# Two column groups of an output projection as a seven-product pair, woven with the groups around it

## The chip, the cores and the metric

The kernel runs on one core of one Trainium2 chip. The metric is the device time of one execution in microseconds; the time before is the median of three runs. A profile is one further execution, recorded instruction by instruction.

## The reference

One layer of a streaming-encoder trunk on 256 tokens of width 2048, all in float32: a SwiGLU block, LayerNorm, a mixer, LayerNorm, a second SwiGLU block, LayerNorm, and a gated per-layer input. Cut to what matters here, the mixer's end is

```
merged = sigmoid(ga) * (y_m @ w_up_m) + sigmoid(gb) * (y_sb @ w_up_sb)   # 256 x 2048
mix    = merged @ w_out                                                  # w_out 2048 x 2048
x      = layer_norm(ALPHA * x + mix, ln2_g, ln2_b)
x      = layer_norm(ALPHA * x + 0.5 * swiglu(x), ln3_g, ln3_b)
```

## The kernel before

**Matmuls.** Tokens lie in two halves of 128 (t = 0, 1). The width is handled in column groups of 512 and the contracted dimension in chunks of 512, each chunk as two weight tiles of 256 rows. A *unit* (the main loop, L1301 to L1329) is one weight tile against one token half: six matmuls of 128 x 512, because both operands are split into a high part (type float32r) and a low part, the rest, and three of the four cross products are kept (L1319 to L1321), for each of two blocks of 128 rows.

**Weights.** A weight tile is loaded from memory into a `raw` tile (SP's queue, L1238, 512 KB). ScalarE casts it into the high part (L1264), VectorE subtracts to get the low part (L1268). This *split* runs some weights ahead; `HELD` says for each mode how many raw tiles and how many splits may be held, and near a stage boundary `SPLIT_EDGE` allows 11 splits.

**Activations.** A finished 128 x 512 tile is turned by four transposes on TensorE (L293), then cast by ScalarE (L295) and subtracted by VectorE (L300). An `ActT` holds the turned tiles.

**Plain groups and pairs.** `group` makes a plain column group: 8 weight tiles, each used by two units, 16 units. `seven` makes a *pair*: two column groups at once with seven products where the plain way has eight. In a chunk, tokens, contracted rows and columns each have two halves; sums of quarters of the activations (the *forms*) are multiplied with sums of quarters of the weights. A chunk needs seven units, each with a weight of its own to split, so that a pair has 28 units. The weight sums are made in place on the raw tiles: on VectorE (`plus`, L366) or by a load from memory that adds to what lies there (`plus_load`, issued by GpSimd, L372). `both7` combines the products on VectorE (L420, L426) and ScalarE (L436, L439). The forms are made by `form_turn`: four VectorE operations of 128 x 256 (L310 to L314), then two casts on ScalarE (L287) and two subtractions on VectorE (L288) for each chunk; for them a whole copy of the turned tile is kept (L299).

**Order.** The program is a list of units and of other steps, laid out in Python. `weave` puts a side list evenly between the units of a main list. What follows a unit's last matmul (`done`) is issued at once; later steps go to a planner (`Sched`) with a due time in planned microseconds, such as `DELAY["form"]`. Each engine then takes its queue in that order, and waits where something is not there yet.

**The stretch in question.** The last woven part ends with `ups(2)`. Then come `bring_back` (the residual rows return from memory, four loads of 512 KB), the turns of the first three merged groups, and:

```
    program.extend(ups(3))
    ...
    for g in range(4):
        pairs = group(w_out, range(0, D, 2 * P), g * COL, COL, mergedT, out_done(g))
        if g == 3:
            program.extend(flat(pairs[:-SKEW]) + skewed(pairs[-SKEW:]))
        else:
            program.extend(flat(pairs))
        if g == 1:
            program.append(norm2.load)
```

`ups(3)` is the last group of the two up projections (16 units); `up_done` multiplies by the gate (L1068), adds the two branches (L1070) and, for g = 3, plans its turn. `out_done` adds a group of `mix` to the residual rows (L1123) and takes LayerNorm statistics (L496). After the last group `Norm.finish` aggregates (L502), normalises (L508), and `Norm.turn` transposes the rows (L519) for the second SwiGLU. `skewed` puts the last six weight tiles' first token half ahead of the second, so that the first half can be normalised early.

Of the kernel before, what the change touches and what calls it, by code (L numbers as in the profile page):

```python
# [13 lines left out]
P = 128  # L14
S = 256
TT = S // P
D = 2048
# [6 lines left out]
COL = 512  # L24
# [2 lines left out]
TEMP_BUFS = 6  # L27


HELD = {"ffn": (11, 6), "mix": (6, 6), "woven": (9, 6), "wide": (11, 6)}  # L30
RAW_EDGE, SPLIT_EDGE = 4, 11
EDGE = 6

AHEAD = 3
PSUM_BUFS = 8
SKEW = 6

HEAD = 20

# [67 lines left out]
class ActT:  # L107


    def __init__(self, alloc, forms=None, later=False):  # L110
        self.alloc, self.soon = alloc, forms is not None and not later
        self.forms, self.whole = forms, {}
        self.tiles = {}
        self.left = {}

    def get(self, c, tt):
        if (c, tt) not in self.tiles:
# [62 lines left out]
def flat(pairs):  # L180
    return [u for p in pairs for u in p]


def skewed(pairs):
    return [p[0] for p in pairs] + [p[1] for p in pairs]
# [3 lines left out]
def kernel(  # L189
# [7 lines left out]
    x, out = x[0], out[0]  # L197
    p = p[0, 0]
    w_in, w_out, w_up_m, w_up_sb = w_in[0], w_out[0], w_up_m[0], w_up_sb[0]
# [9 lines left out]
    sched = Sched()  # L209
    temps = [0]  # L210

    def temp():
        sched.until(lambda: temps[0] < TEMP_BUFS)
        temps[0] += 1
        return temp_pool.tile([P, COL], F32, name="temp", tag="temp")

    def drop(n=1):
        temps[0] -= n
# [71 lines left out]
    def transposed(src, act, c, t):  # L290
        ps = misc([P, 4, P])
        for k in range(4):
            nc.tensor.transpose(ps[:, k], src[:, k * P:(k + 1) * P], ident[:])  # L293
        dst = act.get(c, t)
        nc.scalar.copy(dst[:, 0], ps[:])  # L295
        if act.soon:
            if c not in act.whole:
                act.whole[c] = big()
            nc.scalar.copy(act.whole[c][:, t * COL:(t + 1) * COL], ps.rearrange("q k s -> q (k s)"))  # L299
        nc.vector.tensor_tensor(out=dst[:, 1], in0=ps[:], in1=dst[:, 0], op=ALU.subtract)  # L300
        act.mark(c, t, 4)
        if act.soon and all(act.ready(c, h) for h in range(TT)):
            sched.spawn(form_turn(act, c), DELAY["form"] + 5.0 * c)

    def form_turn(act, c):

        a = [act.whole[c][:, t * COL:(t + 1) * COL] for t in range(TT)]
        s12, s34 = temp(), temp()
        l, r = slice(0, 2 * P), slice(2 * P, 4 * P)
        nc.vector.tensor_tensor(out=s12[:, l], in0=a[1][:, r], in1=a[1][:, l], op=ALU.subtract)  # L310
        nc.vector.scalar_tensor_tensor(out=s12[:, r], in0=s12[:, l], scalar=-1.0, in1=a[0][:, l],  # L311
                                       op0=ALU.mult, op1=ALU.subtract)
        nc.vector.tensor_tensor(out=s34[:, l], in0=a[0][:, l], in1=a[1][:, l], op=ALU.subtract)
        nc.vector.tensor_tensor(out=s34[:, r], in0=a[0][:, r], in1=s12[:, r], op=ALU.add)  # L314
        yield 4.0
        for h, src in enumerate((s12, s34)):
            dst = act.forms.get(c, h)
            split_psum(dst[:, 0], dst[:, 1], src.rearrange("q (k s) -> q k s", s=P))
            drop()
            act.forms.mark(c, h, 4)  # L320
# [18 lines left out]
    def group(w, rows, col0, cols, act, done):  # L339

        accs = [{} for _ in range(TT)]
        pairs = []
        for i, r in enumerate(rows):
            tile = plain(rows_of(w, r, col0, cols))
            pairs.append([Unit(tile, t, accs[t], act, r // COL, r % COL // P,
                               i == 0, i == len(rows) - 1, done) for t in range(TT)])
        return pairs
# [59 lines left out]
    def in_line(pairs):  # L407

        out = []
        for head, first, then in pairs:  # L410
            at = max(len(out) - 4, 0)
            out = out[:at] + head + out[at:] + first + then
        return out

    def both7(w, ca, cb, act, dest, ready, loaded):

        r, held = {}, {}

        def put(k, t, a, b, op):
            nc.vector.tensor_tensor(out=r[k, t], in0=a, in1=b, op=op)  # L420

        def rest():
            u = r[0, 1]
            put(0, 1, held[7], u, ALU.add)
            z = r[1, 1] = dest(1, 1)
            nc.vector.scalar_tensor_tensor(out=z, in0=u, scalar=-1.0, in1=held[5],  # L426
                                           op0=ALU.mult, op1=ALU.subtract)
            ready(1, 1)
            return
            yield  # L430

        def done(m, ps):
            held[m] = ps
            if m == 1:
                r[0, 1] = dest(0, 1)
                nc.scalar.copy(r[0, 1], ps)  # L436
            elif m == 2:
                r[0, 0] = dest(0, 0)
                nc.scalar.copy(r[0, 0], ps)  # L439
                ready(0, 0)  # L440
            elif m == 6:
                r[1, 0] = dest(1, 0)
                put(0, 1, ps, r[0, 1], ALU.add)
                put(1, 0, held[5], r[0, 1], ALU.add)
                sched.spawn(rest(), DELAY["rest"])
            elif m == 4:
                sched.until(lambda: (1, 1) in r)
                put(0, 1, ps, r[0, 1], ALU.add)
                ready(0, 1)
            elif m == 3:  # L450
                put(1, 0, ps, r[1, 0], ALU.subtract)
                ready(1, 0)

        return seven(w, ca, w, cb, D, COL, act, done, loaded)

    program = []

    def mode(name):
        program.append(Mode(name))
# [6 lines left out]
    class Norm:  # L466
# [47 lines left out]
        def turn(self, t, c):  # L514

            xs, act = xres(t, c * COL), self.act
            ps = misc([P, 4, P])
            for k in range(4):
                nc.tensor.transpose(ps[:, k], xs[:, k * P:(k + 1) * P], ident[:])  # L519
            if act.soon:  # L520
                if c not in act.whole:
                    act.whole[c] = big()
                whole = act.whole[c][:, t * COL:(t + 1) * COL]
            else:
                whole = temp()[:]
            whole = whole.rearrange("q (k s) -> q k s", s=P)
            for k in range(4):
                i = 4 * c + k
                activate(whole[:, k], ps[:, k], ACT.Identity, scale=self.gb[:, i:i + 1], bias=self.gb[:, 16 + i:17 + i])
            dst = act.get(c, t)  # L530
            split_psum(dst[:, 0], dst[:, 1], whole)
            act.mark(c, t, 4)
            if not act.soon:
                drop()
            elif all(act.ready(c, h) for h in range(TT)):
                sched.spawn(form_turn(act, c), DELAY["form"] + 5.0 * c)
            sched.spawn(self.affine(t, c), self.wait[0] + self.wait[1] * (2 * c + t))
            return
            yield
# [506 lines left out]
            yield from stick(h)  # L1046


    mergedT = ActT(act_tile)
    ga0 = sq0 + 3 * HS * DS  # L1050
    gt = {}

# [30 lines left out]
    def ups(g, swap=False):  # L1083
        parts = [flat(group(w_up_m, range(0, HM * DM, 2 * P), g * COL, COL, ymT, up_done(g, 0, swap))),
                 flat(group(w_up_sb, range(0, HS * DS, 2 * P), g * COL, COL, ysbT, up_done(g, 1, not swap)))]
        if swap:
            parts.reverse()
        return parts[0] + parts[1]

    every = (range(4), range(4))  # L1090
# [10 lines left out]
    def pair(g):  # L1101
# [6 lines left out]
    mode("woven")  # L1108
    program.extend(weave(main, in_line([both7(w_in, sq0 + 2 * HS * DS, sq0 + 2 * HS * DS + COL, x1T, sv_dest, sv_ready, later),
                                   both7(w_in, 3072, 3072 + COL, x1T, mo_dest, mo_ready, every), pair(1), pair(2), pair(3)])))  # L1110
    mode("mix")
    program.append(bring_back)
    program.append(lambda: [sched.spawn(merge_turn(g, t), 1.0 + 2.0 * g + t) for g in range(3) for t in range(TT)])
    program.extend(ups(3))

    x2T = ActT(act_tile, ActT(act_tile))
    norm2 = Norm(ln2_g[0], ln2_b[0], x2T, ALPHA, (4.0, 1.0))

    def out_done(g):
        def done(ps, t):  # L1120
            assert (t, g) in norm1.whole
            xs = xres(t, g * COL)
            nc.vector.scalar_tensor_tensor(out=xs, in0=xs, scalar=ALPHA, in1=ps, op0=ALU.mult, op1=ALU.add)  # L1123
            norm2.chunk(t, g)
        return done

    for g in range(4):
        pairs = group(w_out, range(0, D, 2 * P), g * COL, COL, mergedT, out_done(g))
        if g == 3:
            program.extend(flat(pairs[:-SKEW]) + skewed(pairs[-SKEW:]))  # L1130
        else:
            program.extend(flat(pairs))
        if g == 1:
            program.append(norm2.load)

    boundary("ffn")

# [163 lines left out]
    for u in program:  # L1301
# [14 lines left out]
        for k in range(2):  # L1316
            hi, lo = a[:, 0, u.sub + k], a[:, 1, u.sub + k]
            first, last = u.start and k == 0, u.stop and k == 1
# [38 lines left out]
```

## Time and profile before

| | |
|---|---|
| median of three runs | 2167.06 us (2166.25 to 2169.68) |
| the profiled execution | 2169.55 us, of it a span of 2167.7 us |
| TensorE (PE) busy | 2157.4 us of the span |
| VectorE (DVE) busy | 1893.7 us |
| ScalarE (ACT) busy | 1347.1 us |
| moved by DMA | 535.98 MB, mean 247 GB/s |
| first and last w_out load issued | 1243.9 and 1330.5 us |
| first and last addition of `mix` (L1123) | 1307.4 and 1376.8 us |

Times of rows are microseconds from the start of the span. PE is the matmul side of TensorE, PEld its weight loads, which overlap matmuls; POOL is GpSimd, SP the queue that issues loads. A row of the timeline gives the start, the length, the engine, the line, the operation, what is written from what, the shape and the count; in brackets the idle time of the engine before it, and what ended it. Consecutive rows of one engine can overlap by some hundredths, so that the distance between starts is what an operation costs. L12 is line 12 of the kernel before.

### The profile page before, as it was taken

To read this page: it belongs to the slowest core of one execution; us is meant where nothing else is said; L and a number is where in the kernel's file an instruction comes from. 1 tells how busy PE (TensorE), PEld (TensorE's weight loads), DVE (VectorE), ACT (ScalarE), POOL (GpSimd) and SP (SyncE) were. 2 spreads that over 40 slices of the span, in tenths; PEclk is the share of its full clock that TensorE was granted. 3 is DMA by queue.
4 is the path that set the end of the run, shared out by engine and by line. 5 is a ranking of instruction groups with operands and counts; after the bars stand their busy time and mean duration, and the time that the engine had idled before them with its cause. 6 is when DMAs were issued, how large, how long until landed. Compare 5 with 4: busy or idle time off the path is not lost.

```text
span 2167.7 us, 27662 instructions
## 1 busy us (share of the span) xinstructions
PE 2157.4 (100%) x9798; PEld 1783.9 (82%) x9798; DVE 1893.7 (87%) x2088; ACT 1347.1 (62%) x1658; POOL 218.2 (10%) x186
## 2 busy tenths in 40 slices
PE   9999999999999999999999999999999999999999
PEld 7888888888888888888888888888888888888887
DVE  6899999999998898887878975799999999999974
ACT  7656666656655765677866554556556656656572
POOL 0111111111100000101010000011111111111000
PEclk9999999999999999999999999999999999999999
DMA  9899899999994667978898976679989999999642
GB/s 349 215 275 270 249 270 275 272 280 268 266 318 140 215 218 219 242 218 203 260 272 260 273 260 203 201 192 279 267 245 276 279 266 277 257 276 294 237 166 87
DMA packets 283179, 535.98 MB, mean 247 GB/s; under 512 B 17144, under 2 KB 34464, under 8 KB 283040
## 3 DMA queue, kind: packets, MB, share of 16 engines
q1 hardware_dynamic: 234624, 440.87, 59.9%
q0 software_dynamic: 48416, 93.33, 23.9%
q8 instruction: 77, 1.26, 0.2%
q14 instruction: 62, 0.51, 0.1%
HBM read 527.85 MB, written 6.29 MB: 246 GB/s over the span
## 4 chain that ended last, share of the span: by engine, by line
PE 93%; issue 2%; DMA 2%; DVE 2%; ACT 0%; POOL 0%; SPq 0%; POOLq 0%; DVEq 0%; ACTq 0%
PE mm L1319 30%; PE mm L1321 30%; PE mm L1320 30%; DMA raw<-in_ffn_w_dram 2%; PE ms L293 1%; DVE split L1268 1%; PE ms L519 0%; DVE raw L366 0%; PE ms L984 0%; PE ms L906 0%; PE ms L921 0%; PE ms L997 0%; POOL raw L372 0%; PE ms L1008 0%; DMA actT<-ymaway 0%
## 5 line engine op out<-in xcount | busy, mean ns | idle before, releaser
L1264 ACT CAST split<-raw 128x1024 fp32r<-128x1024 f32 (+1 forms) x1089 | 1089.4, 1044 | 513.8 <-DMA raw<-in_ffn_w_dram 172.7
L1268 DVE TENSOR_TENSOR split<-raw,split 128x1024 fp32r<-128x1024 f32 (+1 forms) x1089 | 1277.8, 1212 | 141.5 <-ACT split L1264 134.6
L1319 PE MATMUL mm<-split,actT 128*128 128x512 f32 x3064 | 1203.0, 393 | 1.2 <-DVE big L420 1.2
L1321 PE MATMUL mm<-split,actT 128*128 128x512 f32 x3064 | 1189.5, 388 | 0.6 <-DVE actT L300 0.6
L1320 PE MATMUL mm<-split,actT 128*128 128x512 f32 x3064 | 1188.4, 388 | 1.0 <-DVE split L1268 1.0
L1321 PEld LDWEIGHTS mm<-split,actT 128*128 128x128 f32 x3064 | 575.8, 188 | 120.7 <-DVE actT L300 1.4
L1320 PEld LDWEIGHTS mm<-split,actT 128*128 128x128 f32 x3064 | 576.6, 188 | 115.9 <-DVE split L1268 3.4
L1319 PEld LDWEIGHTS mm<-split,actT 128*128 128x128 f32 x3064 | 576.3, 188 | 115.5 <-issue 2.6
L372 POOL DMA_DIRECT2D raw<-in_ffn_w_dram x140 | 169.7, 1441 | 1204.9 <-DVE split L1268 809.6
L366 DVE TENSOR_TENSOR raw<-raw 128x1024 f32<-128x1024 f32 x190 | 231.6, 1220 | 1.6
L372 POOL DMA_DIRECT2D raw<-in_w_in_dram x38 | 46.0, 1426 | 505.7 <-DVE split L1268 432.5
L295 ACT CAST actT<-ms 128x512 fp32r<-128x512 f32 x60 | 35.1, 586 | 77.7 <-PE ms L293 73.2
L644 DVE SCALAR_TENSOR_TENSOR big<-mm,big 128x512 f32<-128x512 f32 x112 | 76.5, 685 | 2.9 <-PE mm L1321 2.8
L592 DVE TENSOR_TENSOR temp<-mm,temp 128x512 f32<-128x512 f32 x108 | 73.1, 686 | 1.8 <-PE mm L1321 0.6
L300 DVE TENSOR_TENSOR actT<-ms,actT 128x512 fp32r<-128x512 f32 x60 | 41.1, 687 | 16.5 <-ACT big L299 11.0
L243 ACT ACTIVATE temp<-mm 128x512 f32<-128x512 f32 (+1 forms) x36 | 20.3, 570 | 49.5 <-PE mm L1321 49.5
L239 ACT ACT_TABLE_LOAD x34 | 43.6, 1283 | 0.6
L288 DVE TENSOR_TENSOR actT<-temp,actT 128x512 fp32r<-128x512 f32 x40 | 26.5, 689 | 17.3 <-ACT actT L287 17.2
L1180 DVE TENSOR_TENSOR temp<-temp,big 128x512 f32<-128x512 f32 (+1 forms) x10 | 5.8, 583 | 26.4 <-ACT temp L243 26.4
L287 ACT CAST actT<-temp 128x512 fp32r<-128x512 f32 x40 | 23.9, 620 | 8.0 <-DVE temp L311 7.4
L243 ACT ACTIVATE rstd<-mv,eps 128x1 f32<-128x1 f32 x6 | 1.8, 295 | 41.8 <-DVE mv L502 41.8
L1123 DVE SCALAR_TENSOR_TENSOR big<-big,mm 128x512 f32<-128x512 f32 x8 | 5.5, 686 | 25.3 <-PE mm L1321 25.3
(133 smaller groups left out, 605.6 us busy)
## 6 DMA issues: line engine op xcount, KB each, us to landing
raw<-in_ffn_w_dram SPq DMA_DIRECT2D x527, 512.0 KB, 6.9
raw<-in_w_in_dram SPq DMA_DIRECT2D x144, 512.0 KB, 5.3
raw<-in_ffn_w_dram POOLq DMA_DIRECT2D x140, 512.0 KB, 9.8
raw<-in_w_in_dram POOLq DMA_DIRECT2D x38, 512.0 KB, 9.0
raw<-in_w_out_dram SPq DMA_DIRECT2D x32, 512.0 KB, 5.5
raw<-in_w_ple_gate_dram SPq DMA_DIRECT2D x32, 512.0 KB, 5.2
raw<-in_w_in_dram SPq DMA_DIRECT2D x56, 256.0 KB, 3.8
raw<-in_w_up_m_dram SPq DMA_DIRECT2D x16, 512.0 KB, 6.8
```

What stands on the lines that cost most here:

```text
L239: nc.scalar.preload_act_table_set(table[0])
L295: nc.scalar.copy(dst[:, 0], ps[:])
L300: nc.vector.tensor_tensor(out=dst[:, 1], in0=ps[:], in1=dst[:, 0], op=ALU.subtract)
L366: nc.vector.tensor_tensor(out=out.tile[:, :, :cols], in0=a.tile[:, :, :cols], in1=b.tile[:, :, :cols], op=ALU.add)
L372: nc.gpsimd.dma_start(out=out.tile[:, :, :cols], in_=src, accum_op=ALU.add)
L592: nc.vector.tensor_tensor(out=out, in0=a, in1=b, op=op)
L644: nc.vector.scalar_tensor_tensor(out=xs, in0=ps, scalar=0.5, in1=xs, op0=ALU.mult, op1=ALU.add)
L1264: nc.scalar.copy(hi[:, ks], r[:, ks])
L1268: nc.vector.tensor_tensor(out=lo[:, ks], in0=r[:, ks], in1=hi[:, ks], op=ALU.subtract)
L1319: nc.tensor.matmul(ps, hi, w[0][:, k, :u.cols], start=first, stop=False, skip_group_check=u.onto)
L1320: nc.tensor.matmul(ps, hi, w[1][:, k, :u.cols], start=False, stop=False, skip_group_check=u.onto)
L1321: nc.tensor.matmul(ps, lo, w[0][:, k, :u.cols], start=False, stop=last, skip_group_check=u.onto)
```

## The change

The four column groups of w_out are no longer four plain groups. Groups 0 and 1 become a pair on `mergedT`, which for that gets forms. The first eight units of `ups(3)` run as before; the other eight, group 2, and the first two weight tiles of group 3 are woven one to one with the 28 units of the pair; the last six weight tiles of group 3 follow, skewed as before. The loads of the LayerNorm weights move behind group 2. In each chunk the two weight sums of the second and third product are made by accumulating loads and the other two on VectorE. The combined products go through temporary tiles, from which `out_done` adds them to the residual rows. The forms of `mergedT` are planned 3.0 + 0.5 c after a chunk c is turned (`OUT_FORM`), and the mode is a new one, "out", with up to 9 raw tiles and 6 splits held, before 6 and 6.

```diff
+HELD = {..., "out": (9, 6)}
+OUT_HEAD, OUT_FORM = 8, (3.0, 0.5)
 ...
-            sched.spawn(form_turn(act, c), DELAY["form"] + 5.0 * c)
+            sched.spawn(form_turn(act, c), act.gaps[0] + act.gaps[1] * c)
 ...
-    mergedT = ActT(act_tile)
+    mergedT = ActT(act_tile, ActT(act_tile))
+    mergedT.gaps = OUT_FORM
 ...
-    mode("mix")
+    mode("out")
     program.append(bring_back)
     program.append(lambda: [sched.spawn(merge_turn(g, t), 1.0 + 2.0 * g + t) for g in range(3) for t in range(TT)])
-    program.extend(ups(3))
 ...
-    for g in range(4):
-        pairs = group(w_out, range(0, D, 2 * P), g * COL, COL, mergedT, out_done(g))
-        ...
+    sums = {}
+
+    def out_dest(k, t):
+        sums[k, t] = temp()
+        return sums[k, t][:]
+
+    def out_ready(k, t):
+        out_done(k)(sums[k, t][:], t)
+        drop()
+
+    last = group(w_out, range(0, D, 2 * P), 3 * COL, COL, mergedT, out_done(3))
+    main = (ups(3) + flat(group(w_out, range(0, D, 2 * P), 2 * COL, COL, mergedT, out_done(2))) + [norm2.load]
+            + flat(last[:-SKEW]))
+    side = in_line([both7(w_out, 0, COL, mergedT, out_dest, out_ready, every)])
+    program.extend(main[:OUT_HEAD] + weave(main[OUT_HEAD:], side) + skewed(last[-SKEW:]))
```

More of the change, by code (lines that the diff above doesn't have):

```diff
@@ L27 @@
 TEMP_BUFS = 6
-HELD = {"ffn": (11, 6), "mix": (6, 6), "woven": (9, 6), "wide": (11, 6)}
+HELD = {"ffn": (11, 6), "mix": (6, 6), "woven": (9, 6), "wide": (11, 6), "out": (9, 6)}
 RAW_EDGE, SPLIT_EDGE = 4, 11
@@ L114, in __init__ @@
         self.left = {}
+        self.gaps = DELAY["form"], 5.0
     def get(self, c, tt):
@@ L535, in turn @@
             elif all(act.ready(c, h) for h in range(TT)):
-                sched.spawn(form_turn(act, c), DELAY["form"] + 5.0 * c)
+                sched.spawn(form_turn(act, c), act.gaps[0] + act.gaps[1] * c)
             sched.spawn(self.affine(t, c), self.wait[0] + self.wait[1] * (2 * c + t))
@@ L1125, in out_done @@
         return done
-    for g in range(4):
-        pairs = group(w_out, range(0, D, 2 * P), g * COL, COL, mergedT, out_done(g))
[L1129 to L1134, printed above, removed]
+    sums = {}
[10 more added lines that the diff above has]
+    program.extend(main[:OUT_HEAD] + weave(main[OUT_HEAD:], side) + skewed(last[-SKEW:]))
     boundary("ffn")
```

## The prediction

> **What bounds the kernel now.** I read the page's busy table and the chain that ended last, then the stretches of time around the change, then single rows of each engine's timeline.
>
> ```profile
> span 2167.7 us, 27662 instructions
> PE 2157.4 (100%) x9798; PEld 1783.9 (82%) x9798; DVE 1893.7 (87%) x2088; ACT 1347.1 (62%) x1658; POOL 218.2 (10%) x186
> PE 93%; issue 2%; DMA 2%; DVE 2%; ACT 0%; POOL 0%; SPq 0%; POOLq 0%; DVEq 0%; ACTq 0%
> 0.00:20.00 20.00, 17.98 (x77) 14.77 (x78) 9.10 (x13) 10.59 (x16) 0.99 (x7) 1.00 0.89 319
> 300.00:600.00 300.00, 300.00 (x1341) 248.54 (x1340) 282.74 (x280) 186.26 (x197) 46.04 (x38) 1.00 0.96 274
> 1260.00:1400.00 140.00, 140.00 (x649) 115.50 (x648) 91.60 (x111) 74.16 (x105) 0.00 (x0) 1.00 0.67 223
> 1400.00:1430.00 30.00, 30.00 (x134) 24.83 (x133) 29.76 (x45) 13.93 (x18) 2.44 (x2) 1.00 0.51 148
> ```
>
> The page's rows say that TensorE is busy all the time and carries 93% of the chain, so a matmul fewer is worth its own duration, as long as nothing else becomes late. The stretches (columns: stretch, length, PE, PEld, DVE, ACT, POOL, clock, DMA share, GB/s) show what there is to hide work behind. In 1260 to 1400, the end of the mixer that is changed, PE has no idle time, VectorE is busy 91.6 of 140 us and DMA 0.67. VectorE is the engine next to the bound: 282.7 of 300 us in the first SwiGLU, 29.76 of 30 just behind the changed stretch. So the question is whether VectorE can take what the pair hands it.
>
> **The matmuls removed.** Four plain column groups are 4 x 16 units of six matmuls; now two groups (32 units) and a pair (4 chunks x 7 products = 28) are 60. Four units go, and the built program has indeed 24 matmuls fewer, no transpose more.
>
> ```profile
> 1362.65 0.39 PE L1319 MATMUL mm<-split,actT 128*128 128x512 f32 x1
> ...
> 1366.05 0.39 PE L1319 MATMUL mm<-split,actT 128*128 128x512 f32 x1
> 148.69 0.44 PE ms L293 x4
> ```
>
> Between the two matmul rows lie 15 matmuls in 3.40 us: 0.2267 us each, 1.36 a unit, so 24 x 0.2267 = **5.4 us saved**. The last row, from the chain, is a set of four transposes: 0.44 us. I count units from the first one of the last up group: that group, the two plain groups and the pair are 76 units, before 80.
>
> **What VectorE and ScalarE get.** Each product has a weight of its own to split: 28 splits where the two groups had 16, so 12 more on ACT (L1264) and DVE (L1268); 8 weight sums on DVE (L366), the other 8 by accumulating loads; four form turns, each four small DVE operations (L310 to L314) and two ACT casts and two DVE subtractions (L287, L288); eight ACT copies of the turned tiles (L299); 6 combinations of products (L420, L426). For ACT that is 12 x 0.96 + 18 x 0.5 = 21 us more on 74 of 140: it lies beside other work and costs nothing except where a cast waits.
>
> ```profile
> 1246.64 9.17 DVE L1268 TENSOR_TENSOR split<-raw,split 128x1024 fp32r<-128x1024 f32 x8
> 1262.80 0.69 DVE L1068 TENSOR_TENSOR big<-mm,big 128x512 f32<-128x512 f32 x1
> 1263.52 0.69 DVE L1070 TENSOR_TENSOR big<-big 128x512 f32<-128x512 f32 x1
> 1264.13 1.22 DVE L1268 TENSOR_TENSOR split<-raw,split 128x1024 fp32r<-128x1024 f32 x1
> 1407.88 0.42 DVE L310 TENSOR_TENSOR temp<-big 128x256 f32<-128x256 f32 x1
> ...
> 1409.35 2.36 DVE L1268 TENSOR_TENSOR split<-raw,split 128x1024 fp32r<-128x1024 f32 x2
> 1411.62 1.29 DVE L288 TENSOR_TENSOR actT<-temp,actT 128x512 fp32r<-128x512 f32 x2
> 1412.82 1.23 DVE L1268 TENSOR_TENSOR split<-raw,split 128x1024 fp32r<-128x1024 f32 x1
> ```
>
> Back to back a split or a weight sum costs (9.17 - 1.22) / 7 = 1.136; a 512-wide operation 0.72 if the next one needs its result (1262.80 to 1263.52), else 0.61 (1263.52 to 1264.13); a form turn's four 1.47 (1407.88 to 1409.35); two L288 1.20. The sum for DVE is (12 + 8) x 1.136 + 4 x (1.47 + 1.20) + 6 x 0.66 = 37.4 us; 91.6 + 37.4 = 129 of now 134.6 us. On average it fits; but the queue is in order, and work comes in lumps. I followed the built order of DVE's queue and found two places where PE waits for it.
>
> **First place: the last up group's turn.** PE needs that group's two sums (L1070) for its transposes, which stand behind unit 24. The first eight units are ups; from then on up units and pair units alternate.
>
> ```profile
> 1262.62 0.60 PE L293 MATMUL ms<-ident,big 128*128 128x128 f32 x4
> 1263.25 0.59 ACT L295 CAST actT<-ms 128x512 fp32r<-128x512 f32 x1 [0.68 <-PE ms L293]
> 1265.08 0.59 ACT L295 CAST actT<-ms 128x512 fp32r<-128x512 f32 x1 [1.24 <-PE ms L293]
> 1265.56 1.06 ACT L1264 CAST split<-raw 128x1024 fp32r<-128x1024 f32 x1
> 1266.91 0.59 ACT L295 CAST actT<-ms 128x512 fp32r<-128x512 f32 x1 [0.29 <-PE ms L293]
> 1267.39 1.15 ACT L243 ACTIVATE big<-big 128x512 f32<-128x512 f32 x2
> 1284.65 0.69 DVE L1068 TENSOR_TENSOR big<-mm,big 128x512 f32<-128x512 f32 x1 [4.29 <-PE mm L1321]
> DMA to landing us min/median/max: 7.5/10.1/12.1
> DMA to landing us min/median/max: 9.9/11.5/13.2
> ```
>
> PE: from 1262.62 (behind unit 1) six sets of transposes and 23 units, 6 x 0.44 + 23 x 1.36 = 33.9: ready at 1296.5. DVE: the first pair weight's split starts where before's did, at 1264.13, and ends at 1265.35; then POOL issues the accumulating load onto it. Such loads landed in 7.5, 10.1, 12.1 us (shortest, median, longest in 1100 to 1215, last but one row): at 1272.9, 1275.5, 1277.5. ACT casts the sum, 1.05 (L1264): 1273.9, 1276.5, 1278.5. DVE itself is not there sooner than 1275.1: from 1263.25 ACT has now ten turn operations of 0.48 (1265.08 to 1265.56), a cast of 0.96, two sigmoids of 0.5 and 0.9 of waiting for the second set of transposes, so the next cast starts at 1270.9 and ends at 1271.9, and DVE does that split, one form turn and one subtraction behind it (1.14 + 1.47 + 0.61). From there to the end of the group's first L1070, DVE's order holds 11 splits and 2 sums (14.8), three L1068 and the L1070 (0.61 + 0.61 + 0.72 + 0.69 = 2.6), two form turns (2.9), six L288 (3.6): 23.9. So 1299.0, 1300.4 or 1302.4 against 1296.5: **2.5, 3.9 or 5.9 us late**. Before, DVE had waited 4.29 us for PE at this L1068; that slack is gone. I take 3.9, the median load. The ups' last turn then has one more short wait: a PSUM bank that the first of the two sets held is free only when its L300 has run behind a split, 0.6 by the same order.
>
> **Second place: the first LayerNorm turn.** Its transposes stand behind unit 73 and need the normalised rows (L508).
>
> ```profile
> 1366.25 0.69 DVE L1123 SCALAR_TENSOR_TENSOR big<-big,mm 128x512 f32<-128x512 f32 x1 [6.56 <-PE mm L1321]
> 1366.97 0.69 DVE L496 BATCH_NORM_STATS2 stats<-big 128x6 f32<-128x512 f32 x1
> 1378.22 0.26 DVE L502 BATCH_NORM_AGGREGATE mv<-stats 128x2 f32<-128x24 f32 x1
> 1379.05 1.92 DVE L508 TENSOR_SCALAR big<-big,mv,rstd 128x512 f32<-128x512 f32 x4
> ```
>
> DVE's last wait is for the matmuls of the pair's product 6, at the end of unit 46. From there to the second L508 it has 20 splits and 2 sums (25.0), seven L1123 with L496 (7 x 1.33 = 9.3), six L420 and L426 (4.0), 0.2 for the small copy, 0.83 from L502 to L508 and 0.92 for two L508: 40.2 us. PE has 27 units and a small transpose, 36.8: **3.4 us late**. Before, DVE stood idle 6.56 us ahead of that L1123, so nothing was lost there.
>
> **DMA and queues.** SP issues as many loads as before, some w_out loads earlier; the LayerNorm loads move behind the pair. POOL gets eight accumulating loads.
>
> ```profile
> q1 hardware_dynamic: 234624, 440.87, 59.9%
> q0 software_dynamic: 48416, 93.33, 23.9%
> 1204.66 2.42 POOL L372 DMA_DIRECT2D raw<-in_w_in_dram  x2 [10.09 <-DMA raw<-in_w_in_dram]
> 1424.46 2.44 POOL L372 DMA_DIRECT2D raw<-in_ffn_w_dram  x2 [217.38 <-DVE temp L583]
> ```
>
> POOL has nothing else between 1204 and 1424, so nobody queues behind it. 93.33 MB are 178 accumulating loads: 0.239 x 2167.7 / 178 = 2.91 us of all engines each, 23.3 for eight, which brings the stretch from 0.67 to about 0.84; the first SwiGLU runs at 0.96 without PE waiting. I cost it at nothing. If that cover is gone, it shows in the landing time of the first pair, below.
>
> **The sum**: -5.4 + 3.9 + 0.6 + 3.4 = +2.5 us. Against the profiled execution (2169.55 us with a span of 2167.7) 2172.1; against the median of the runs, 2167.06, **2169.6**.
>
> **Rivals.**
> *VectorE keeps up.* If the lumps fall where DVE has slack, the matmuls saved are all there is: 2167.06 - 5.4 = 2161.6. For it speaks the sum over the stretch, 129 of 134.6, and the first SwiGLU, where the same kind of pair runs beside plain groups at 94% of DVE; against it, that both waits are in-order queues with no gap left. Chance 0.08.
> *The first accumulating loads land late* (the slower one). They gate ACT's queue, the form casts behind it and so DVE; past 8.7 us after issue each us costs one. In 1440 to 1444 the longer of two took 13.2 (last row of that fence): 1265.35 + 13.2 + 1.05 + 23.9 = 1303.5, 7.0 late, so -5.4 + 7.0 + 0.6 + 3.4 = +5.6: 2172.7. It passes 0.2% from 11.9 us on. For it: four residual tiles come back in the same microseconds. Against: the stretch's DMA share of 0.67. Chance 0.24.
> *The backlog goes on into the second SwiGLU*, where DVE has 0.24 us free in 30: another wait like the second place, +2.5 + 3.4 = +5.9, 2173.0. Against: there DVE first waits for ACT's casts of the new activations, which takes a backlog up. Chance 0.06.
> *The clock falls in the wait.* In 0 to 20 us PE was idle for 2.0 us and the granted clock stayed 1.00; a wait of 3.4 us in one piece has no row here. If the matmuls then ran at half speed for as long, 1.7 us would be added: +4.2, 2171.3, at the edge of 0.2%. Chance 0.05.
> The Trainium skill, "TensorE: Matmul & The Clock Gate", section "Part 1: The HAM clock gate", states this rule: the array drops to half its clock after an idle window of about 3.4 us. By that rule the second place would sit just on the edge; this trace, with 1.00 through short gaps, does not decide it.
> That the pair is not built is excluded by the count of matmuls.
>
> **How the numbers follow.** A measurement of this kernel tells about 0.2%, 4.3 us, from no change. The forecast (between -2.3, the early load and no second wait, and +4.3) has 0.57. Slower takes late loads, the backlog and half of the clock case: 0.24 + 0.06 + 0.03 = 0.33; faster 0.08; the rest, 0.57 + 0.02 = 0.59, is within. The range: below, -2.3 less the 0.8 by which the fastest run (2166.25) lies under the median: 2164.0; above, late loads and the clock together, +5.6 + 1.7: 2174.4.
>
> **What would show it.** In the profile of after: no PE wait before unit 14; PE waiting 2 to 6 us in all between unit 14 and the transposes of the last up group, released by DVE (L288, L1070); a wait of about 3.4 us on L508 ahead of the first LayerNorm transposes; DVE without idle time from unit 46 to there; 24 matmuls fewer. It is wrong if DVE waits for PE at L1123 as before, if PE waits for a raw load, or if the granted clock leaves 1.00.

## The result, and the profile after

The changed kernel takes 2171.19 us (median of 19 runs, 2168.7 to 2174.22), the kernel before 2167.21 on the same chip: a ratio of **1.0016, 95% interval [1.001, 1.0022]**, 3.5 us. Measured once more later it was 1.0015 [1.0006, 1.0024]. The forecast was 2169.6 (2164.0 to 2174.4), "within 0.2%" at 0.59. The total is right; its terms are not, as two profiles of the same changed kernel show.

The first lines of the page of after: the span, the engines' busy time, the chain that ended last by engine.

```profile
span 2167.9 us, 27733 instructions
PE 2153.5 (99%) x9774; PEld 1779.6 (82%) x9774; DVE 1931.2 (89%) x2138; ACT 1367.3 (63%) x1688; POOL 227.9 (11%) x194
PE 96%; DVE 2%; ACT 1%; issue 1%; DMA 0%; SPq 0%; DVEq 0%; ACTq 0%
```

Here are 24 matmuls fewer, but TensorE is no longer busy all the time. The waits of TensorE from 1255 to 1400 (line that waited, what it waited for, us in total, times, longest) and then the stretches:

```profile
PE ms L521 <- DVE big L510: 2.9, 1, 2.9
PE ms L295 <- DVE big L1073: 2.1, 1, 2.1
```
```profile
1260.00:1400.00 140.00, 134.89 (x610) 110.10 (x609) 126.24 (x159) 90.86 (x131) 9.70 (x8) 0.98 0.80 240
1280.00:1300.00 20.00, 17.83 (x77) 14.02 (x76) 19.86 (x25) 13.10 (x17) 2.42 (x2) 0.96 0.89 242
1360.00:1380.00 20.00, 17.05 (x76) 13.83 (x75) 15.15 (x23) 5.48 (x12) 0.00 (x0) 0.91 0.66 237
1400.00:1430.00 30.00, 30.00 (x134) 24.86 (x133) 29.76 (x44) 15.61 (x20) 2.44 (x2) 1.00 0.50 152
```

(Line numbers of after are those of before plus 2 to 5 up to L1125, and plus 9 in the main loop: L1070 is now L1073, L508 is L510, L293 is L295.) Those are the two places of the prediction, and no other. But the granted clock, the share of full speed that the trace records for TensorE, is 0.96 and 0.91 in just the two stretches that hold them. Single rows of TensorE behind the two waits show what that is:

```profile
1297.70 0.66 PE L295 MATMUL ms<-ident,big 128*128 128x128 f32 x4 [2.15 <-DVE big L1073]
...
1298.51 0.63 PE L1329 MATMUL mm<-split,actT 128*128 128x512 f32 x1
1298.94 0.63 PE L1330 MATMUL mm<-split,actT 128*128 128x512 f32 x1
...
1301.84 0.39 PE L1328 MATMUL mm<-split,actT 128*128 128x512 f32 x1
1370.49 1.11 PE L521 MATMUL ms<-ident,big 128*128 128x128 f32 x4 [2.95 <-DVE big L510]
```

From one start to the next are 0.43 us, where the prediction's rows had 0.227: matmuls at half clock, until 1301.5. The transposes at 1370.49 take 1.11 instead of 0.60.

I measure the stage from the last up group's first transposes to the eighth set of LayerNorm transposes, where both kernels do the same but for the change. Before: 1262.62 to 1388.62, 126.00 us. After: 1260.98 to 1390.37, 129.39, which is **+3.39**. The second profile of the same changed kernel, taken later, has the same two waits and no half clock at all; its stage is 127.06, **+1.06**:

```profile
1280.00:1300.00 20.00, 17.85 (x80) 14.15 (x79) 19.90 (x25) 11.89 (x15) 2.42 (x2) 1.00 0.90 242
1360.00:1380.00 20.00, 17.05 (x83) 13.81 (x83) 16.08 (x25) 6.12 (x15) 0.00 (x0) 1.00 0.75 263
```
```profile
1299.14 0.66 PE L295 MATMUL ms<-ident,big 128*128 128x128 f32 x4 [2.15 <-DVE big L1073]
...
1299.86 0.39 PE L1329 MATMUL mm<-split,actT 128*128 128x512 f32 x1
1300.09 0.40 PE L1330 MATMUL mm<-split,actT 128*128 128x512 f32 x1
...
1303.34 0.50 PE L1328 MATMUL mm<-split,actT 128*128 128x512 f32 x1 [0.33 <-DVE actT L302]
1370.92 0.66 PE L521 MATMUL ms<-ident,big 128*128 128x128 f32 x4 [2.95 <-DVE big L510]
```

So the stage costs 1.06 us in one execution and 3.39 in another with equal waits; the 2.33 between them are the half clock, 1.0 between the stage's start and the LayerNorm transposes and 1.3 behind these. Outside the stage the span of one execution differs from that of another by some 3 us (the first profile of after is 3.2 us shorter there than the profile of before), so spans are not compared below, but stages and medians.

### The profile page after: what moved, and what is told of

Same layout as the page of the kernel before. It is cut to its first block, busy times and chain, and to the rows that moved or that the text cites. A ratio compares the mean times of both kernels' runs of the same rounds, so it can differ in the third digit from the quotient of the medians.

```text
span 2167.9 us, 27733 instructions
## 1 busy us (share of the span) xinstructions
PE 2153.5 (99%) x9774; PEld 1779.6 (82%) x9774; DVE 1931.2 (89%) x2138; ACT 1367.3 (63%) x1688; POOL 227.9 (11%) x194
## 4 chain that ended last, share of the span: by engine, by line
PE 96%; DVE 2%; ACT 1%; issue 1%; DMA 0%; SPq 0%; DVEq 0%; ACTq 0%
PE mm L1328 31%; PE mm L1330 31%; PE mm L1329 31%; DVE split L1277 1%; PE ms L295 1%; PE ms L521 1%; ACT split L1273 0%; PE ms L986 0%; PE ms L908 0%; PE ms L923 0%; PE ms L999 0%; DMA raw<-in_ffn_w_dram 0%; DVE raw L368 0%; PE ms L1010 0%; ACT L241 0%
## 5 line engine op out<-in xcount | busy, mean ns | idle before, releaser
L1273 ACT CAST split<-raw 128x1024 fp32r<-128x1024 f32 (+1 forms) x1101 | 1101.0, 1044 | 505.1 <-DMA raw<-in_ffn_w_dram 175.2
L1277 DVE TENSOR_TENSOR split<-raw,split 128x1024 fp32r<-128x1024 f32 (+1 forms) x1101 | 1292.3, 1211 | 137.3 <-ACT split L1273 128.7
L368 DVE TENSOR_TENSOR raw<-raw 128x1024 f32<-128x1024 f32 x198 | 241.2, 1220 | 1.7
L302 DVE TENSOR_TENSOR actT<-ms,actT 128x512 fp32r<-128x512 f32 x60 | 41.2, 686 | 17.3 <-ACT big L301 10.7
L290 DVE TENSOR_TENSOR actT<-temp,actT 128x512 fp32r<-128x512 f32 x48 | 31.7, 687 | 17.4 <-ACT actT L289 17.3
L289 ACT CAST actT<-temp 128x512 fp32r<-128x512 f32 x48 | 28.4, 619 | 8.1 <-DVE temp L313 7.4
L245 ACT ACTIVATE temp<-ms,gbT 128x128 f32<-128x128 f32 x64 | 24.1, 460 | 5.6 <-PE ms L521 5.6
L295 PEld LDWEIGHTS ms<-ident,temp 128*128 128x128 f32 x176 | 21.7, 140 | 5.9 <-DVE actT L302 0.4
## 6 DMA issues: line engine op xcount, KB each, us to landing
raw<-in_ffn_w_dram POOLq DMA_DIRECT2D x140, 512.0 KB, 10.1
```

Source lines behind the costliest of these rows:

```text
L245: nc.scalar.activation(out, in_, func, **kw)
L368: nc.vector.tensor_tensor(out=out.tile[:, :, :cols], in0=a.tile[:, :, :cols], in1=b.tile[:, :, :cols], op=ALU.add)
L1273: nc.scalar.copy(hi[:, ks], r[:, ks])
L1277: nc.vector.tensor_tensor(out=lo[:, ks], in0=r[:, ks], in1=hi[:, ks], op=ALU.subtract)
```

## The experiments

Theory A: VectorE makes TensorE wait at two places, and behind each wait the matmuls run at half clock for some microseconds. Rivals: the clock is innocent, and the matmuls behind the waits are slow for another reason; the landing of the accumulating loads, not VectorE, sets the first place; the matmuls saved don't show because something else bounds the stage.

**Dummy matmuls in the two waits** (label warm).

```
     ps = misc([P, 4, P])
+    for _ in range(9 if act is mergedT and (c, t) == (3, 0) else 0):     # 12 ahead of the LayerNorm turn
+        nc.tensor.matmul(ps[:, 0], ones[:], ones[:], start=True, stop=True)
     for k in range(4):
         nc.tensor.transpose(ps[:, k], src[:, k * P:(k + 1) * P], ident[:])
```

> The kernel after, with 9 fp32 matmuls of ones (128x128) queued just ahead of the last up group's last chunk of transposes (token tile 0) and 12 just ahead of the first LayerNorm transposes, into the PSUM bank that the transposes then overwrite: TensorE works where it stood still for 2.1 and 2.9 us, and nothing of the result changes. Theory A (two waits for VectorE, and after each some 3 to 4 us of matmuls at half clock): the following work still starts as late, with at most 1 us of wait left at each place, but the matmuls behind both keep their 0.227 us, so 1.9 + 1.6 = 3.5 us come off the kernel after: about 2167.7, 0.9984 of it. Rival (the waits alone; the slower matmuls behind them come from something else, such as the work beside them): pitch 0.42 to 0.43 us stays for some 9 matmuls behind each place, and the time is 2171 or, if the dummies overrun the waits, up to 2172.

Measured: 1.0011 [1.0002, 1.002], stage 127.09. The granted clock was 1.00 in every stretch, the pitch 0.23 us, and 0.3 us of wait was left at the second place. The work behind both places started as late as before, and the stage fell by 2.30 us, not 3.5: 0.97 to the LayerNorm transposes and 1.33 behind them. The first half clock had cost less than I had added up, in part because a wait of 0.33 us for a PSUM bank (L302, in the second profile of after above; 0.6 us from start to start) is covered by slow matmuls and comes back without them. That the stage equals the one of after without half clock (127.06) puts a price on it twice.

**After and the dummies once more, side by side** (after2, warm2).

> The kernel after as it is, once more, beside the run that follows it on the same chip: 1.0016 of before as measured first, the two waits of 2.1 and 2.9 us for L1073 and L510, and half clock behind the second in every profile, behind the first in most.

> The kernel with 9 and 12 dummy matmuls in the two waits once more, on the same chip as the kernel after. In the stage from the last up group's first transposes to the last LayerNorm transposes the first profiles gave 129.39 us for the kernel after and 127.09 for this one. Theory A (half clock has its price, of which VectorE gives back a part): the median lies 2.3 us under the kernel after's of this call, and the stage is 127 us again. Rival (clock innocent, the profiles' difference is chance): the medians agree within 0.7 us.

Measured: after 2170.80 us, 1.0015 [1.0006, 1.0024]; with dummies 2169.67, 1.0007 [0.9998, 1.0016], stage 127.06. The expectation for after was wrong: this is the profile shown above, with the waits and no half clock. The medians differ by 1.1 us, between what the two theories gave, and the intervals overlap. The mean granted clock that is on record for every execution tells more. Of the 30 executions of after in both measurements, 18 have 0.998 or 0.997, as the first profile has; the 22 with dummies, and the 82 of the kernel before that ran beside these and the other experiments, all have 0.999 or 1.000. (Half clock behind one wait alone can still read 0.999, as in the profile of edge8 below.) In the first measurement the 14 executions of after at 0.998 or less have a median of 2171.7 us and the other 5 of 2169.3; in the second it is 2172.4 for 4 and 2170.4 for 7. So half clock comes in most executions, not in all, and costs 2.1 to 2.5 us, as the stage said.

**Fewer splits ahead of the second boundary** (edge8), and **the same with dummies at the first place** (edge8warm).

```
-            return RAW_EDGE, SPLIT_EDGE
+            return RAW_EDGE, SPLIT_EDGE if j < edges[1] - EDGE else 8
```

> The kernel after, with the limit of weight splits done ahead of the second SwiGLU's boundary set to 8 instead of 11 (the first boundary as it was): VectorE has three splits of 1.14 us fewer in its queue ahead of the first LayerNorm turn. Theory A: the second wait of TensorE, 2.9 us on L510, goes or falls below 1 us, and the half-clock matmuls behind it (1.6 us) go with it, unless the later splits make TensorE wait behind the boundary; the first wait (2.1 us) and its half clock stay: 2167 to 2168, 3 to 4.5 us under the kernel after. Rival (the splits are wanted as soon as they are there): the second wait moves behind the boundary, and the time stays at 2171. Rival (clock innocent): 2.9 us gained at most, slow matmuls still there.

> The kernel with the limit of 8 splits ahead of the second boundary, and the 9 dummy matmuls ahead of the last up group's last transposes (the result does not change). It differs from the run with the limit of 8 alone in the clock behind the first wait only. Theory A: without the half clock TensorE is 1.9 us earlier behind the first place; VectorE is then the later one at the first LayerNorm turn and gives back some 0.7: about 1.2 us under the run with the limit of 8, 0.9997 of before. Rival (clock innocent): no difference, 1.0003 of before.

Measured: edge8 1.0003 [0.9994, 1.0012] with a stage of 125.60 (-0.40), and edge8warm 1.0003 [0.9994, 1.0012] with 124.65 (-1.35). The second wait is gone and does not come back behind the boundary, so the splits were not wanted there yet; the first is as it was, 2.15, with half clock behind it in that profile. Dummies at the first place take another 0.95 us off the stage. The medians, 0.63 and 0.45 us above those of before measured beside them (2168.80 against 2168.17, 2167.53 against 2167.08), can't tell that microsecond. They also hold something that the expectation left out: the edit lowers the limit at the boundary behind the second SwiGLU too, and there, at 2065 us, TensorE waits 1.26 us for L510 (none in after), outside the stage.

**The small form operations on GpSimd** (pool): in `form_turn`, for this pair alone, five GpSimd operations instead of VectorE's four (GpSimd does not get the fused one).

> The kernel after, with the four small operations of each of the pair's four form turns given to GpSimd (as five there): 4 x 1.47 = 5.9 us leave VectorE, and the subtractions that need their result now wait for GpSimd. Theory A: two of those turns lie ahead of the last up group's sums in VectorE's queue, 2.9 us, so the first wait (2.1 us on L1073) and the half clock behind it (1.9 us) go; the second wait is counted from VectorE's last idle moment, behind all turns, and stays at 2.9 + 1.6: about 2167.2, 4 us under the kernel after. Rival (the accumulating load's landing sets the first place): the wait stays at 2 us or so, and the time at 2171. If GpSimd is slower at them than VectorE's other work covers, VectorE waits for GpSimd instead and the first wait stays or grows.

Measured: 1.0026 [1.0015, 1.0038], stage 132.54 (+6.54), the slowest of all, though VectorE has 5.9 us less to do. The first wait did not go. TensorE's three longest waits in the stage, then two of GpSimd's rows and the mean split of VectorE while GpSimd works (1306 to 1315), then the mean split of after in the same stretch:

```profile
PE mm L1335 <- DVE split L1283: 3.1, 3, 1.2
PE ms L527 <- DVE big L516: 3.0, 1, 3.0
PE ms L296 <- DVE big L1079: 2.1, 1, 2.1
```
```profile
1275.87 1.72 POOL L316 TENSOR_TENSOR temp<-big 128x256 f32<-128x256 f32 x1
1277.67 0.74 POOL L317 TENSOR_TENSOR temp<-temp,big 128x256 f32<-128x256 f32 x1
L1283 DVE TENSOR_TENSOR split<-raw,split 128x1024 fp32r<-128x1024 f32 x5 | 8.6, 1762 | 0.1
```
```profile
L1277 DVE TENSOR_TENSOR split<-raw,split 128x1024 fp32r<-128x1024 f32 x6 | 7.1, 1220 | 0.3 <-ACT split L1273 0.3
```

GpSimd operations of the same shape take 0.74 us or 1.72, a turn 6.1 (1269.09 to 1275.17) where VectorE takes 1.47, and while GpSimd works VectorE's splits take 1.76 instead of 1.22 and two subtractions for the forms up to 2.38 instead of 1.29: VectorE gives back there what it was spared. One accumulating load that is issued by 1269.7 in after stands behind these turns until 1287.00. The Trainium skill, "SBUF — State Buffer", section "SBUF: two separate sides", says that the two engines lock a shared pair of ports against each other for a whole instruction where a VectorE operation reads two operands from SBUF; these rows agree with that.

**GpSimd forms, weave after 6 units, 9 splits** (pool_h6e9).

> Small form operations of the pair on GpSimd, the weave begun after 6 units of the last up group instead of 8, and a split limit of 9 instead of 11 ahead of the second SwiGLU's boundary. Theory A: both waits of TensorE go or stay under 0.5 us, the clock stays at 1.00, and what is left is the 24 matmuls fewer: 2167.1 - 5.4 = 2161.7, 9 us under the kernel after and 0.9975 of the kernel before. Rival (the matmuls saved don't turn up in the time, because something else in the stretch is the bound): 2165 to 2167 even without the two waits. If only one wait goes: about 2166.

Measured: 0.9995 [0.9986, 1.0004], stage 123.18 (-2.82). Clock 1.00 throughout; the waits are 0.7 and three of 0.3. So in the stage about half of the matmuls saved turns up once the waits shrink, but 5.4 us were expected: I had left out small waits of 1.6 us in all, and what GpSimd costs VectorE. The median (2167.25 us against 2168.17) is only 0.9 us under before, a time that the rival gave too; the stage alone speaks against it here, and h7e9f1 below does so with its median.

**The order alone** (h7e9, then h7e9f1 with earlier form turns).

```
-OUT_HEAD, OUT_FORM = 8, (3.0, 0.5)
+OUT_HEAD, OUT_FORM = 7, (3.0, 0.5)      # h7e9f1: 7, (1.0, 0.5)
...
-            return RAW_EDGE, SPLIT_EDGE
+            return RAW_EDGE, SPLIT_EDGE if j < edges[1] - EDGE else 9
```

> The kernel after with two constants changed and nothing moved to GpSimd: the weave begins after 7 units of the last up group instead of 8 (OUT_HEAD), and the limit of splits ahead of the second SwiGLU's boundary is 9 instead of 11. Theory A: one split less stands ahead of the last up group's sums in VectorE's queue, so the first wait falls from 2.1 to about 1.0 us; two splits (2.3 us) and the first place's rest less ahead of the first LayerNorm turn, so the second falls from 2.9 to under 0.7 us; both too short for the half clock (1.2 us had none in the run with the form operations on GpSimd). -5.4 + 1.0 + 0.6 and up to 0.6 of small waits: about 4 us under before, 0.998 to 0.9985 of it. If the half clock still comes behind the first wait: 0.9993. Rival (the saving is lost to something else than these waits): 1.000 or above.

> The weave after 7 units, 9 splits ahead of the second boundary (as in the run before), and the pair's form turns begun 1.0 us after their chunk's transposes instead of 3.0 (OUT_FORM). In the run before, TensorE waited 1.1 us at the pair's first form (L290, whose ScalarE cast came late in its queue), 0.9 at the last up group's sums and 0.3 for a bank. Theory A: the 1.1 us goes, the others stay: 1.1 us less than that run, about 2164.9 against a before of 2167.1, 0.9988 of before, and no half clock anywhere in the stage. Rival (the earlier form turns push the splits behind them, and the first wait grows by as much): no better than 0.9993.

Measured: h7e9 0.9993 [0.9984, 1.0002], stage 123.63 (-2.37); h7e9f1 **0.9985 [0.9976, 0.9994]**, 2164.29 us against 2167.88, stage 122.26 (-3.74). It is faster than both kernels. TensorE's waits in h7e9:

```profile
PE mm L1330 <- DVE actT L290: 1.1, 1, 1.1
PE ms L295 <- DVE big L1073: 0.9, 1, 0.9
PE mm L1328 <- DVE actT L302: 0.3, 1, 0.3
```

and in h7e9f1, with the stretch from 1260 to 1400:

```profile
PE ms L295 <- DVE big L1073: 0.7, 1, 0.7
PE mm L1328 <- DVE actT L302: 0.3, 1, 0.3
```
```profile
1260.00:1400.00 140.00, 138.94 (x641) 113.93 (x640) 131.80 (x166) 97.51 (x139) 9.70 (x8) 1.00 0.85 254
```

The second wait is gone, the first is 0.7 to 0.9 us, too short for the clock. The 1.1 us at the pair's first form was not foreseen for h7e9 and goes with the earlier form turn. VectorE works 131.8 of 140 us in the fastest kernel, some of it already the next stage's, and 126.2 in after: it was not the sum over the stage that was too much.

**Without VectorE's weight sums** (nosums).

> The kernel after without the 8 sums of weights that VectorE makes for the pair (products 6 and 4 of each chunk then use other weights, so half of the pair's output is not the reference's; the matmuls, splits and loads are as they were). 8 x 1.14 = 9.1 us leave VectorE: two sums stand ahead of the last up group's turn, two in the count to the first LayerNorm turn. Theory A: the first wait (2.1) goes, the second falls from 2.9 to about 0.6, no half clock: -5.4 + 0.6 = 4.8 us under before, 0.9978 of it. Rival (the accumulating loads' landing holds the first place, DMA the rest): first wait still about 2 us, time no better than 0.9995 of before.

Measured: 0.9986 [0.9978, 0.9995], stage 123.48 (-2.52). VectorE is what holds TensorE: the waits fall to these, and the clock stays at 1.00.

```profile
PE ms L296 <- DVE big L1076: 0.9, 1, 0.9
PE ms L524 <- DVE big L513: 0.7, 1, 0.7
PE mm L1331 <- DVE actT L303: 0.3, 1, 0.3
```

The second is as expected, the first should have gone. What is next in line there is the landing of an accumulating load:

```profile
1278.66 1.05 ACT L1276 CAST split<-raw 128x1024 fp32r<-128x1024 f32 x1 [4.45 <-DMA raw<-in_w_out_dram]
...
1279.74 1.23 DVE L1280 TENSOR_TENSOR split<-raw,split 128x1024 fp32r<-128x1024 f32 x1 [0.97 <-ACT split L1276]
```

With one sum less behind it, VectorE comes early to this split and waits 0.97 us for ScalarE's cast, which waited 4.45 us for the load. In after the same cast ended at 1277.83, and VectorE came at 1278.54. So of the 2.3 us that the two sums take, about 1.0 goes to the load; whether an earlier landing would have helped was not tried.

**Pauses of known length in the kernel before** (ladder, ladder2).

```
+    nc.tensor.matmul(ps[:, 0], ones[:], ones[:], start=True, stop=True)
+    for _ in range(n):
+        nc.gpsimd.memset(ones[:], 1.0)
+    nc.tensor.matmul(ps[:, 0], ones[:], ones[:], start=True, stop=True)
```

> The kernel before, with 12 pauses of TensorE put just ahead of single sets of transposes in the two SwiGLUs and the mixer: a small matmul reads the tile of ones, GpSimd writes ones into it again n times (n = 2 to 24 in shuffled order), and a second small matmul waits for that (the result does not change). It shows after which waits the matmuls run at half clock, with no change of the kernel's schedule. Theory A: waits of about 2 us and more, whatever their cause, are followed by matmuls 0.43 us apart for 2 to 4 us, waits of 1.2 us and less are not; near 2 us either can be. Rival (the clock falls only behind waits of 3.4 us or more, and in the kernel after it fell for another reason): no slow matmuls behind pauses of 2 to 3 us. Either way the time goes up by the sum of the pauses, some 10 to 40 us.

> The kernel before with 22 pauses ahead of every second set of transposes, of 7 to 12 writes by GpSimd in shuffled order, so most waits lie between 1.9 and 3.4 us (some longer, where GpSimd is late). The first row of pauses had half clock behind none of 0.64, 1.17, 1.69 and 2.74 us and behind all eight from 3.72 to 7.62 us; in the kernel after it came behind 2.15 and 2.95. Theory B (how the wait lies against a window of time decides, and a wait that fills the larger part of one is enough): some of the waits between 2 and 3.4 us have half clock behind them and others of the same length have not, the share rising with the length. Rival (a fixed length decides): a length below which none and above which all have it, in which case 2.15 us in the kernel after needs another reason than its length.

Measured, over both (34 pauses): half clock behind none of the 3 waits up to 1.69 us, 1 of 4 from 1.95 to 2.21, 5 of 6 from 2.48 to 2.74, 2 of 4 from 2.81 to 3.26, and all 17 from 3.72 us on. It lasted until 2.7 to 6.1 us after the wait's end. Two neighbours of the second kernel:

```profile
1313.89 0.49 PE L300 MATMUL ms<-ones 128*128 128x128 f32 x2 [2.21 <-POOL ones L299]
...
1314.89 0.40 PE L1329 MATMUL mm<-split,actT 128*128 128x512 f32 x1
1319.35 0.49 PE L300 MATMUL ms<-ones 128*128 128x128 f32 x2 [2.48 <-POOL ones L299]
...
1320.45 0.63 PE L1329 MATMUL mm<-split,actT 128*128 128x512 f32 x1
```

A wait of 1.95 us had it once and twice not; one of 3.11 us had it not. So a fixed length does not decide. What decides is how a wait lies on a grid of time that the traces' own clock record shows. Five profiles (both pause kernels, the first of after, edge8, pool) have 29 spells of half clock between them; each lasts 3.41, 6.83 or, once, 10.24 us, and within a profile every one starts a whole multiple of 3.41 us after the first entry of the record. Here are stretches of that grid around the two waits, in the first profile of after and then in the second (columns as in the prediction: stretch, length, PE, PEld, DVE, ACT, POOL, clock, DMA share, GB/s):

```profile
1294.91:1298.32 3.41, 1.26 (x8) 0.81 (x7) 3.38 (x5) 1.04 (x2) 0.00 (x0) 1.00 1.09 213
1298.32:1301.73 3.41, 3.41 (x10) 2.63 (x9) 3.38 (x5) 2.02 (x3) 0.00 (x0) 0.50 1.07 310
1366.59:1370.00 3.41, 0.95 (x5) 0.45 (x3) 2.94 (x6) 0.64 (x2) 0.00 (x0) 1.00 0.92 343
1370.00:1373.41 3.41, 2.92 (x9) 2.54 (x10) 2.94 (x5) 2.33 (x6) 0.00 (x0) 0.50 0.03 10
```
```profile
1294.02:1297.43 3.41, 2.97 (x14) 2.12 (x12) 3.41 (x4) 2.94 (x3) 0.72 (x1) 1.00 1.00 188
1297.43:1300.84 3.41, 1.70 (x10) 1.49 (x11) 3.35 (x5) 1.01 (x3) 0.00 (x0) 1.00 1.08 231
1365.70:1369.11 3.41, 2.28 (x11) 1.54 (x9) 3.38 (x6) 0.00 (x0) 0.00 (x0) 1.00 1.05 384
1369.11:1372.52 3.41, 1.59 (x9) 1.42 (x10) 2.98 (x8) 2.13 (x5) 0.00 (x0) 1.00 0.55 202
```

In the first profile the waits leave 2.15 and 2.46 us of one stretch without matmuls, and the next stretch runs at half clock. In the second the same waits of 2.15 and 2.95 us are divided over two stretches each, which leaves at most 1.71 and 1.82 us in one, and the clock stays. Over all profiles of this case, a stretch at full clock with 2.02 us or more without matmuls was followed by half clock each time (27 of 27), one with 1.73 us or less never, and of five with 1.81 to 1.95 us two were. So theory B stands, whatever engine the wait is for: a wait between 2 and 3.3 us has half clock behind it in one execution and not in another, by how it falls on the grid.

## Why the prediction was right, and where only the total was

Step by step, as the prediction put it:

- **Matmuls, -5.4 us: right.** The stage holds 498 matmuls of 128 x 512 instead of 522, at 0.227 us, and the fastest version shows 3.7 of the 5.4 us in the stage.
- **VectorE's sum: right within 3 us.** 129 us were forecast for the 140; it is 126.2 and, in the second profile, 127.4. ScalarE, DMA (0.80 and 0.81; 0.84 forecast) and the queues cost nothing in after: TensorE waits for none of them.
- **First place: right place and cause, 4.5 us forecast, waits of 2.15 + 0.33 measured.** From start to start, as the prediction counts, these are 2.3 and 0.6 us. The count of VectorE's queue was exact: 23.9 us forecast from the split to the first L1073, and the rows give 1273.61 to 1297.64, 24.0.

```profile
1273.61 1.22 DVE L1277 TENSOR_TENSOR split<-raw,split 128x1024 fp32r<-128x1024 f32 x1
...
1296.95 0.69 DVE L1073 TENSOR_TENSOR big<-big 128x512 f32<-128x512 f32 x1
```

  What was mis-sized is its start. The first row is ScalarE's wait in 1262 to 1300, the second the landing of the accumulating loads issued up to 1275:

```profile
ACT split L1273 <- DMA raw<-in_w_out_dram: 4.4, 2, 4.0
DMA to landing us min/median/max: 7.4/12.6/16.5
```

  I took the median landing of the accumulating loads, 10.1 us; the first one landed in 7.4, so that ScalarE waited only 0.4 us for it, and VectorE's own order set the time: the low end of the three, 2.5. The bank's 0.6 was right.

- **Second place: 3.4 forecast, a wait of 2.95 measured, 3.1 from start to start.** From L422 at 1330.40 to the start of the transposes at 1370.49 are 40.1 us against 40.2 forecast. In this two small errors cancel: the forecast counted two L508, but the transposes began behind the first of the four L510 (ended 1370.43), and the rest of the count was some 0.2 us short. TensorE arrived 0.3 us later than 27 units and a transpose, half of it because a wait is counted from the end of the last matmul (0.39), not from the next start (0.227).
- **The rival "the clock falls in the wait", 0.05 and 1.7 us: this is the step that failed.** It was given to the second wait alone, and argued from a row that can't bear it: the clock column of 0 to 20 us reads 1.00, but the matmuls there are 0.43 us apart until 10.2 us, ahead of the first entry of the trace's clock record:

```profile
8.93 0.63 PE L1319 MATMUL mm<-split,actT 128*128 128x512 f32 x1
9.36 0.63 PE L1320 MATMUL mm<-split,actT 128*128 128x512 f32 x1
```

  In fact both waits can have it, by how they fall on the grid of 3.41 us, and when it came it took 2.3 us. The clock off 1.00 was also one of the prediction's own signs of being wrong. The Trainium skill, "TensorE: Matmul & The Clock Gate", section "Part 1: The HAM clock gate", has the clock halved after at least one idle window of about 3.4 us, and calls the window free-running. The second agrees with the grid of 3.41 us in these traces; the first is not borne out here, since 2.02 us without matmuls in a stretch were enough, and 8 of 14 waits between 1.95 and 3.26 us.
- **VectorE keeps up: refuted** for this order, by both waits. **Late loads: not seen in the two profiles of after, but near.** ScalarE did wait 4.0 us for a later accumulating load, and VectorE came to that split without a wait, with 0.7 us to spare in the first profile and 2.1 in the second. **Backlog into the second SwiGLU: refuted**, TensorE is busy 30.00 of 30 us in 1400 to 1430.

From start to start the parts are -5.4 + 2.3 + 0.6 + 3.1 = +0.6 in the profile without half clock; another 0.5 is spread over slightly longer pitches of the matmuls, and the stage is +1.06. With the half clock it is +3.39. The executions with a mean clock of 0.999 or more lie 2.1 and 2.5 us above before in the two measurements, the others 4.5 and 4.6: so in both groups 1.0 to 1.4 us more than the stage shows lie outside it, and their cause stays open. That the forecast of +2.5 came within 1 us of the measured +3.5 is therefore partly luck: the first place cost 1.6 us less than its 3.9, and what made up for it were the half clock, which the sum left out, and the part outside the stage.

## What to carry to other kernels

A queue that fits on average may still be late in lumps: take the last moment at which the next engine waited, add up what stands in its queue from there to the wanted result, and compare that with the bound engine's work in the same time. Here that count was right to 0.1 us at the first place and to some 0.2 at the second, and moving one unit of the weave, two splits and a due time recovered what the change had lost (1.0016 to 0.9985), while taking work off VectorE onto GpSimd made it slower. A wait of TensorE of 2 to 3 us should be charged with another 1.0 to 1.3 us for the clock behind it in some of the executions; waits of up to 1.7 us cost only themselves. Where such a wait has to stay, matmuls that nobody needs, put into it, kept the clock. And a constant that is changed for one boundary should be followed to the others that it governs: the limit of 8 cost 1.26 us at the next one.

## What the runs showed of the hardware that was not expected

- The granted clock changes on a grid of 3.41 us: behind a stretch with 2.02 us or more without matmuls it was half (27 of 27), behind one with 1.73 us or less never. So waits of up to 1.69 us had none, those from 1.95 to 3.26 us had it or not by how they fell, and all 17 pauses from 3.72 us had it; matmuls were then 0.43 us apart instead of 0.227, until 2.7 to 6.1 us after the wait.
- Matmuls that nobody needs, put in the wait, held the clock at 1.00 through the stage in both profiles of that kernel, and shortened the stage by 2.3 us against the one with half clock.
- GpSimd operations on 128 x 256 tiles slowed VectorE's splits from 1.22 to 1.76 us, and took 1.72 instead of 0.74 us themselves.
